# The S5 half of an output projection as seven block products per pair of blocks

## The chip, the cores and the metric

One Trainium2 chip, one of its cores. The metric is the device time of one execution in microseconds (us), as the median of several runs. The engines are TensorE (PE, with its weight loads as PEld), VectorE (DVE), ScalarE (ACT), GpSimd (POOL) and SyncE (SP), whose queue issues nearly all transfers.

## The reference

One layer of a hybrid streaming encoder on 512 prompt frames and 32 sample frames, all float32, model width 2048:

```
h = rmsnorm(x, norm1_g);  p = h @ w_in            # q, f, i, g, u: 1024 columns each
o_h = hgrn_mixer(q, f, i, g)                      # 8 heads of 128, gated linear recurrence
hh  = gelu(s5_scan(u))                            # 64 groups, complex diagonal state
o_s = hh * sigmoid(hh @ w_glu + b_glu)            # the gate
x = x + concat(o_h, o_s) @ w_out                  # the output projection
a = relu(rmsnorm(x, norm2_g) @ w_ff1)             # 2048 x 8192
x = x + a*a @ w_ff2
y = rmsnorm(x, final_norm_g)                      # and the mixers' final states
```

The output projection is a 2048 x 2048 product on 544 frames. Its lower 1024 input channels come from the HGRN heads, its upper 1024 from the gate.

## The kernel before

Activations lie transposed: 128 channels on the partitions, the 544 frames (`T`) along the free axis, in two halves of 272 (`HALF`). A float32 product is made of three products in the type float32r: each operand is split into a high part (a cast on ScalarE) and a low part (the difference, on VectorE), and `step` (L120 on) multiplies high by high, high by low and low by high. `split_w` (L105 on) splits a weight tile of 128 x 1024, `split` an activation of 544 columns.

`gemm` (L128 on) makes one block of 128 output rows: per 8 input blocks a weight tile is loaded into the ring `w`, split into the ring `hl` (two buffers each), and 8 steps for either frame half follow, in two of three PSUM banks `g`. A ring hands out tiles of its pools in turn; a tile waits until all users of the tile before it in that buffer are done. After each second step `tick` lets a piece of other work onto TensorE. The instructions of TensorE stand in the order in which the program writes them; on the other engines a planner orders them, by the place in the program and by its own costs. `first()` moves instructions 2000 places ahead; weight loads and splits use it.

The stages around the change:

- The gate, 8 calls of `gemm` on the S5 output (`ht`, eight split tiles of the pool `a`). Each result becomes `sg` (sigmoid, then a multiplication with `hhl`) and is split into one more tile of pool `a`, kept in `mixs`.
- The S5 half of the output projection (the loop over `NK` = 16 blocks before `drain(0)`): x is loaded in two halves into tiles `xr` of the tag `tt`, `gemm([wo[m, 1]], mixs)` makes the product, VectorE adds it (L1028), and SyncE stores the sum to `x2` in DRAM (L1029).
- Beside it runs `hg_head(7)`, the recurrence of the last HGRN head, a generator whose `yield n` says after how many ticks its next piece may come. Its pieces on TensorE: the transposes of vT (3 ticks) and of kT (24 more for this head), the state products, six levels of diagonal products (5 ticks each), then the output product `po` (L805 on), 3 and 8 ticks later, and a column sum 4 ticks after that. Its exponentials and differences lie on ScalarE and VectorE.
- Each head's normalised output goes to DRAM (`mh`). The loop after `hg_out` loads the eight back into `x_tile("mhl")` and splits them into `mix0` to `mix7` (L1039, L1040). `x_tile` draws on four buffers of the tag `x`, which also hold `hhl` before and x after.
- The HGRN half: 16 calls of `gemm([wo[m, 0]], mixh, ...)`, whose result is added to x; then x is multiplied with the norm's weight and turned into the seven forms that the feed-forward layer takes.

The feed-forward layer's `seven` makes a 2 x 2 block product (two block rows of weights, two frame halves) with seven block products instead of eight, on sums of weight blocks (`s` tiles) and the forms made by `forms`; it has five kinds of PSUM banks for its sums, X, F, C, D and E. Its second half runs 64 such pairs of blocks, each seven products of 4 steps.

Of the kernel before, what the change touches and what calls it, by code (L numbers as in the profile page):

```python
# [37 lines left out]
class Build:  # L38
# [52 lines left out]
    def ring(self, tag, shape=(128, 1024), dt=F32):  # L91

        turn, parts = self.rings[tag]
        self.rings[tag][0] += 1
        turn %= sum(n for _, n in parts)
        for pool, n in parts:
            if turn < n:
                return pool.tile(list(shape), dt, tag=tag, name=tag, bufs=n)
            turn -= n

    def pair(self):
        t = self.ring("hl", (128, 2, 1024), F32R)
        return t[:, 0], t[:, 1]
# [541 lines left out]
    def hg_head(self, h, q, f, vv, g):  # L645
# [35 lines left out]
        for n, (nm, src, wait) in enumerate((("vT", vv, 3), ("kT", kh, 16 if h < 7 else 24))):  # L681
# [74 lines left out]
        for l, hs in enumerate(levels):  # L756
# [6 lines left out]
            yield 5  # L763
# [87 lines left out]
    def mixers(self):  # L851
# [147 lines left out]
        mixs = []  # L999
        for m in range(8):  # L1000
            t = load_hh(m)
            p = self.gemm([d["wg"][m]], ht)
            sg = self.htmp("sg")
            for h in range(2):
                self.tact(sg[:, HALF * h : HALF * h + HALF], p[h], AF.Sigmoid, bias=c["bglu"][:, m : m + 1])
            for s_, o in nat(t):
                v.tensor_mul(jp(sg[:, o]), jp(sg[:, o]), s_)
            mixs.append(self.split(sg))
# [13 lines left out]
        for m in range(NK):  # L1022
            x = [ms.tile([128, HALF], F32, tag="tt", name="xr", bufs=4) for _ in range(2)]
            for h in range(2):
                nc.sync.dma_start(x[h], d["xT"][:, m, HALF * h : HALF * h + HALF])
            p = self.gemm([wo[m, 1]], mixs, (7,) if m == 0 else ())
            for h in range(2):
                add = lambda h=h, x=x, p=p: v.tensor_add(x[h], x[h], p[h])  # L1028
                store = lambda m=m, h=h, x=x: nc.sync.dma_start(self.x2[m][:, HALF * h : HALF * h + HALF], x[h])  # L1029
                adds.append(add) if (m, h) == (NK - 1, 1) else add()  # L1030
                stores.append(store) if m >= NK - 2 else store()
# [3 lines left out]
        for h in range(8):  # L1035
            t = x_tile("mhl")
            nc.sync.dma_start(t, self.mh[h])
            z = ms.tile([128, 2, T], F32R, tag=f"mix{h}", name=f"mix{h}")
# [22 lines left out]
        for k in range(8):  # L1061
            g = []
            for m in (k, k + 8):
                x = x_tile("x")
                nc.sync.dma_start(x, self.x2[m])
                p = self.gemm([wo[m, 0]], mixh, (), late_adds)
# [22 lines left out]
    def forms(self, q, tmp):  # L1089
# [8 lines left out]
        return b11, t1, t2, b21, t3, b22, t4  # L1098

# [351 lines left out]
```

## Time and profile before

| what | us |
|---|---|
| median of 3 runs (2274.66 to 2280.14) | 2278.12 |
| profiled execution | 2274.9 |
| span of its instructions | 2273.1 |
| S5 half of the output projection, 683.75 to 789.70 | 105.95 |
| HGRN half, 789.70 to 885.50 | 95.80 |

Times in a row are counted from the span's start. "Busy" is the time in which at least one instruction of an engine runs. Neighbouring instructions overlap in the profile (a matmul shows 0.29 us and the next begins 0.125 us later), so the time that one takes from its engine is read from start to start. A wait names the instruction whose end released the waiting one.

### The profile page before, as it was taken

The numbers are of one execution on the slowest core, as the hardware profiler recorded it, in microseconds if no ns is written. First come the engines' busy times: TensorE is split into PE (matmuls) and PEld (weight loads), VectorE is DVE, ScalarE is ACT, GpSimd is POOL, SyncE is SP. The second block draws the span as 40 slices with busy tenths as digits, with TensorE's granted clock in tenths as the row PEclk, the third lists the DMA queues.
The fourth block names the chain that finished last, engine by engine and source line by source line (L and its number), as shares of the span: only waits on it lengthen the run. The fifth ranks groups of instructions, "written<-read, shape, count | busy, mean of one in ns | idle before, by whom it ended". The sixth has DMA issues, their size and how long they took to land.

```text
span 2273.1 us, 46802 instructions
## 1 busy us (share of the span) xinstructions
PE 2243.3 (99%) x19318; PEld 2216.2 (97%) x19318; DVE 1800.8 (79%) x2933; ACT 1289.5 (57%) x2267; POOL 39.1 (2%) x59
## 2 busy tenths in 40 slices
PE   8999999999999999999999999999999999999998
PEld 8999999999999999999999999999999999999998
DVE  7988989887656478777777777778888888888896
ACT  5665666564655265555555555556565565565575
POOL 0010001000000000000000000000000000000000
PEclk9999999999999999999999999999999999999999
DMA  5222232222345565445545444447444344344333
GB/s 196 88 87 89 87 90 87 81 89 86 125 146 173 172 191 177 137 157 179 170 166 181 167 154 152 140 149 260 171 163 163 112 162 165 109 162 172 104 102 107
DMA packets 139927, 322.12 MB, mean 142 GB/s; under 512 B 13345, under 2 KB 66337, under 8 KB 139713
## 3 DMA queue, kind: packets, MB, share of 16 engines
q1 hardware_dynamic: 139072, 316.90, 42.4%
q8 instruction: 151, 2.47, 0.4%
q10 hardware_dynamic: 640, 2.23, 0.3%
q14 instruction: 64, 0.52, 0.1%
HBM read 262.21 MB, written 56.87 MB: 140 GB/s over the span
## 4 chain that ended last, share of the span: by engine, by line
PE 90%; DVE 6%; ACT 2%; DMA 1%; issue 1%; SPq 0%; ACTq 0%; DVEq 0%
PE g L124 9%; PE g L126 9%; PE g L125 8%; PE bX L1140 8%; PE bX L1141 8%; PE bX L1142 8%; PE bE L1141 3%; PE bC L1141 3%; PE bE L1140 3%; PE bC L1140 3%; PE bD L1141 3%; PE bD L1140 3%; PE bF L1140 3%; PE bF L1141 3%; PE bD L1142 3%; PE bE L1142 3%
## 5 line engine op out<-in xcount | busy, mean ns | idle before, releaser
L124 PE MATMUL g<-a,hl 128*128 128x272 f32 x1648 | 491.2, 298 | 6.2 <-ACT hl L108 6.2
L126 PE MATMUL g<-a,hl 128*128 128x272 f32 x1648 | 475.7, 289 | 1.3 <-DVE hl L109 1.3
L125 PE MATMUL g<-a,hl 128*128 128x272 f32 x1648 | 474.7, 288 | 0.0
L109 DVE TENSOR_TENSOR hl<-w,hl 128x1024 fp32r<-128x1024 f32 (+3 forms) x348 | 383.7, 1112 | 107.6 <-ACT hl L108 106.4
L108 ACT CAST hl<-w 128x1024 fp32r<-128x1024 f32 (+3 forms) x348 | 334.6, 962 | 198.8 <-PE g L126 113.7
L109 DVE TENSOR_TENSOR hl<-s,hl 128x1024 fp32r<-128x1024 f32 x256 | 313.1, 1223 | 107.8 <-ACT hl L108 107.5
L108 ACT CAST hl<-s 128x1024 fp32r<-128x1024 f32 x256 | 268.7, 1050 | 179.9 <-PE bD L1142 99.7
L124 PEld LDWEIGHTS g<-a,hl 128*128 128x128 f32 x1648 | 311.7, 189 | 11.4 <-ACT hl L108 6.4
L126 PEld LDWEIGHTS g<-a,hl 128*128 128x128 f32 x1648 | 311.0, 189 | 2.0 <-DVE hl L109 2.0
L125 PEld LDWEIGHTS g<-a,hl 128*128 128x128 f32 x1648 | 311.0, 189 | 0.6 <-DVE a L188 0.2
L1141 PE MATMUL bX<-hf,hl 128*128 128x272 f32 x768 | 222.7, 290 | 0.0
L1141 PE MATMUL bX<-f,hl 128*128 128x272 f32 x768 | 222.6, 290 | 0.0
L1140 PE MATMUL bX<-f,hl 128*128 128x272 f32 x768 | 222.3, 289 | 0.3 <-ACT hl L108 0.3
L1140 PE MATMUL bX<-hf,hl 128*128 128x272 f32 x768 | 222.1, 289 | 0.5 <-ACT bD L1133 0.5
L1142 PE MATMUL bX<-f,hl 128*128 128x272 f32 x768 | 221.7, 289 | 0.8 <-DVE hl L109 0.7
L1142 PE MATMUL bX<-hf,hl 128*128 128x272 f32 x768 | 221.3, 288 | 0.0
L1142 PEld LDWEIGHTS bX<-f,hl 128*128 128x128 f32 x768 | 144.5, 188 | 1.2 <-DVE hl L109 1.2
L1140 PEld LDWEIGHTS bX<-hf,hl 128*128 128x128 f32 x768 | 144.7, 188 | 0.7 <-ACT bD L1133 0.7
L1140 PEld LDWEIGHTS bX<-f,hl 128*128 128x128 f32 x768 | 144.7, 188 | 0.6 <-ACT hl L108 0.5
L1142 PEld LDWEIGHTS bX<-hf,hl 128*128 128x128 f32 x768 | 144.6, 188 | 0.0
L1141 PEld LDWEIGHTS bX<-f,hl 128*128 128x128 f32 x768 | 144.4, 188 | 0.0
L1141 PEld LDWEIGHTS bX<-hf,hl 128*128 128x128 f32 x768 | 144.4, 188 | 0.0
(427 smaller groups left out, 5752.5 us busy)
## 6 DMA issues: line engine op xcount, KB each, us to landing
w<-w SPq DMA_DIRECT2D x256, 512.0 KB, 4.0
w<-wi SPq DMA_DIRECT2D x76, 512.0 KB, 3.4
hd<-ft SPq DMA_DIRECT2D x32, 952.0 KB, 4.7
hf<-hd SPq DMA_DIRECT2D x56, 544.0 KB, 6.1
w<-wo SPq DMA_DIRECT2D x32, 512.0 KB, 3.9
x<-x SPq DMA_DIRECT2D x32, 272.0 KB, 2.8
hhl<-hh SPq DMA_DIRECT2D x16, 274.0 KB, 3.5
x<-xT SPq DMA_DIRECT2D x16, 272.0 KB, 5.0
```

What stands on the lines that cost most here:

```text
L108: self.nc.scalar.copy(hi[:, cols], w[:, cols])
L109: self.last_lo = self.nc.vector.tensor_sub(lo[:, cols], w[:, cols], hi[:, cols].bitcast(F32)).ins.name
L124: te.matmul(o, wh, xh, start=k == 0, stop=False)
L125: te.matmul(o, wh, xl, start=False, stop=False)
L126: te.matmul(o, wl, xh, start=False, stop=k == nk - 1)
L1140: nc.tensor.matmul(b[o], wh[:, s], xh, start=start and k == 0, stop=False, skip_group_check=True)
L1141: nc.tensor.matmul(b[o], wh[:, s], xl, start=False, stop=False, skip_group_check=True)
L1142: nc.tensor.matmul(b[o], wl[:, s], xh, start=False, stop=k == nk - 1, skip_group_check=True)
```

## The change

The S5 half is made by seven products for each pair of output blocks. The gate's results stay whole; from the fifth on, result k and result k + 4 are turned into seven right-hand forms (`right_forms`), split into tiles of pool `a`. For each of 8 pairs `left_forms` makes the sums of the two weight tiles and splits them, and `seven_few` runs seven products of 4 steps in three PSUM banks, copying X into C, F and C again and adding the five results to x on the way. It ticks after each second step. x is now loaded two blocks wide into two tiles `x_tile("xr")` a pair.

The rings in this stage take in tiles that are free then: the weights of odd pairs lie in `mix4` and `mix5`, the sums in `mix6` and `mix7`, a third split buffer in pool `a`. Afterwards the old rings are put back. The first call of the HGRN half leaves the steps of blocks 4 to 7 to its end. In head 7 the transposes of kT come 34 ticks after those of vT and each level after 6.

```
-                return pool.tile(list(shape), dt, tag=tag, name=tag, bufs=n)
+                return pool(turn) if callable(pool) else pool.tile(list(shape), dt, tag=tag, name=tag, bufs=n)
...
-        return t[:, 0], t[:, 1]
+        return t if isinstance(t, list) else (t[:, 0], t[:, 1])
...
-        for n, (nm, src, wait) in enumerate((("vT", vv, 3), ("kT", kh, 16 if h < 7 else 24))):
+        for n, (nm, src, wait) in enumerate((("vT", vv, 3), ("kT", kh, 16 if h < 7 else 34))):
...
-            yield 5
+            yield 5 if h < 7 else 6
...
+        mixf = [[None] * 4 for _ in range(7)]
+        b11s = []
+        def right_forms(k):
+            A, B = slice(0, HALF), slice(HALF, T)
+            x, y = mixs[k], mixs[k + 4]
+            if k % 2 == 0:
+                b11s.append(self.atile())
+            ab, cd, ef = b11s[-1], self.atile(), self.atile()
+            gh = self.atile()
+            o = (A, B)[k % 2]
+            fs = self.forms((x[:, A], x[:, B], y[:, A], y[:, B]),
+                            lambda: ms.tile([128, HALF], F32, tag="tt", name="tt", bufs=4))
+            for f, (z, pair, o) in enumerate(zip(fs, (ab, cd, cd, ef, gh, ef, gh), (o, A, B, A, A, B, B))):
+                hi, lo = pair[0][:, o], pair[1][:, o]
+                a.copy(hi, z)
+                v.tensor_sub(lo, z, hi.bitcast(F32))
+                mixf[f][k] = hi, lo
-            mixs.append(self.split(sg))
+            mixs.append(sg)
+            if m > 3:
+                right_forms(m - 4)
-        for m in range(NK):
-            x = [ms.tile([128, HALF], F32, tag="tt", name="xr", bufs=4) for _ in range(2)]
...
+        mt = lambda h: ms.tile([128, 2, T], F32R, tag=f"mix{h}", name=f"mix{h}")
...
+        self.rings["w"] = [0, [(wpool, 2), (lambda n: flat(mt(4 + n)), 2)]]
+        self.rings["s"] = [0, [(lambda n: flat(mt(6 + n)), 2)]]
+        self.rings["hl"] = [1, [(wpool, 2), (lambda n: hl3, 1)]]
+        for i in range(8):
+            m1 = 2 * i
+            xr = [x_tile("xr").rearrange("q (m t) -> q m t", m=2) for _ in range(2)]
+            for h in range(2):
+                nc.sync.dma_start(xr[h], d["xT"][:, m1 : m1 + 2, HALF * h : HALF * h + HALF])
+            with self.first():
+                r1, r2 = self.load_raw(wo[m1, 1]), self.load_raw(wo[m1 + 1, 1])
+            self.seven_few(self.left_forms(r1, r2), mixf, 4, xr, adds if i == 7 else None)
+            for h in (1, 0):
+                for m in range(2):
+                    store = lambda m=m, h=h, xr=xr, m1=m1: nc.sync.dma_start(
+                        self.x2[m1 + m][:, HALF * h : HALF * h + HALF], xr[h][:, m])
                     stores.append(store) if i == 7 else store()
+        self.rings = rings
-                p = self.gemm([wo[m, 0]], mixh, (), late_adds)
+                p = self.gemm([wo[m, 0]], mixh, (4, 5, 6, 7) if m == 0 else (), late_adds)
+    def left_forms(self, r1, r2):
+        v, sp = self.nc.vector, self.split_w
+        L, H = slice(0, 512), slice(512, 1024)
+        s12, s34 = self.ring("s"), self.ring("s")
+        memo = {}
+        def part(key, n, make):
+            if key not in memo:
+                with self.first():
+                    memo[key] = make()
+            return tuple(x[:, 512 * n : 512 * n + 512] for x in memo[key])
+        def m12():
+            v.tensor_add(s12[:, L], r2[:, L], r2[:, H])
+            v.tensor_sub(s12[:, H], s12[:, L], r1[:, L])
+            return sp(s12)
+        def m34():
+            v.tensor_sub(s34[:, L], r1[:, L], r2[:, L])
+            v.tensor_sub(s34[:, H], r1[:, H], s12[:, H])
+            return sp(s34)
+        mr = lambda: sp(r1)
+        return (lambda: part("r", 0, mr), lambda: part("12", 0, m12), lambda: part("12", 1, m12),
+                lambda: part("r", 1, mr), lambda: part("34", 0, m34), lambda: part("34", 1, m34),
+                lambda: part("22", 1, lambda: sp(r2, None, H)))
+    def seven_few(self, left, right, nk, x, last):
+        X, F, C = (self.gbank() for _ in range(3))
+        add = lambda o, p: v.tensor_add(o, o, p)
+        plan = ((X, True, None), (F, True, None), (X, False, C), (C, False, None), (X, False, F), (F, False, None),
+                (C, False, C))
+        for i, (o, start, copy) in enumerate(plan):
+            if copy is not None:
+                with self.first():
+                    a.copy(copy, X)
+            wh, wl = left[i]()
+            for k in range(nk):
...
+                if k % 2:
+                    self.tick()
+            with self.first():
+                if i == 1:
+                    add(x[1], F.unsqueeze(1).broadcast_to([128, 2, HALF]))
+                if i == 3:
+                    add(x[0][:, 0], C)
+                if i == 5:
+                    add(x[1][:, 0], F)
+        def end():
+            return add(x[0][:, 1], C)
+        with self.first():
+            add(x[1][:, 1], X)
+            if last is None:
+                end()
+            else:
+                last.append(end)
```

## Rows read from the trace of the kernel before

**Rows 1.** The page: busy time, share of the span and instructions of each engine.
```profile
PE 2243.3 (99%) x19318; PEld 2216.2 (97%) x19318; DVE 1800.8 (79%) x2933; ACT 1289.5 (57%) x2267; POOL 39.1 (2%) x59
```
**Rows 2.** Stretches: length, busy (instructions) of PE, PEld, DVE, ACT, POOL; clock, DMA share, GB/s.
```profile
683.75:789.70 105.95, 105.95 (x1033) 103.96 (x1032) 62.17 (x113) 42.66 (x74) 0.00 (x0) 1.00 0.52 167
789.70:885.50 95.80, 95.80 (x769) 95.80 (x768) 71.02 (x143) 54.71 (x97) 0.00 (x0) 1.00 0.59 187
```
**Rows 3.** Timeline of VectorE, S5 half: start, duration, instruction, count, idle time before and releaser.
```profile
768.73 0.44 DVE L1028 TENSOR_TENSOR xr<-xr,g 128x272 f32<-128x272 f32 x1 [0.71 <-PE g L126]
...
774.74 0.44 DVE L1028 TENSOR_TENSOR xr<-xr,g 128x272 f32<-128x272 f32 x1 [0.71 <-PE g L126]
```
**Rows 4.** Waits of TensorE in the whole span: total us, times, longest.
```profile
PE ps L805 <- ACT hgAT L793: 3.0, 1, 3.0
```
**Rows 5.** Stretches of the S5 half with head 7, VectorE alone.
```profile
683.75:704.50 20.75, 19.14 (x33) 1.00 0.60 195
704.50:757.83 53.33, 31.98 (x64) 1.00 0.48 149
```
**Rows 6.** The same stretches, weight splits on VectorE (L109) alone.
```profile
683.75:704.50 20.75, 4.89 (x4) 1.00 0.60 195
704.50:757.83 53.33, 8.55 (x7) 1.00 0.48 149
```
**Rows 7.** The same stretches, additions to x (L1028) alone.
```profile
683.75:704.50 20.75, 2.58 (x6) 1.00 0.60 195
704.50:757.83 53.33, 6.50 (x15) 1.00 0.48 149
```
**Rows 8.** Timeline of VectorE, one pair of the second feed-forward layer.
```profile
1629.56 0.69 DVE L1281 TENSOR_TENSOR s<-w 128x512 f32<-128x512 f32 x1
1630.16 0.69 DVE L1286 TENSOR_TENSOR s<-w 128x512 f32<-128x512 f32 x1
...
1633.84 0.43 DVE L1303 TENSOR_TENSOR acc<-acc,bC 128x272 f32<-128x272 f32 x1
1634.18 0.43 DVE L1303 TENSOR_TENSOR acc<-acc,bX 128x272 f32<-128x272 f32 x1
...
1637.84 1.29 DVE L1176 TENSOR_TENSOR hf<-hf 128x1088 fp32r<-128x1088 f32 x1
1639.05 1.22 DVE L109 TENSOR_TENSOR hl<-s,hl 128x1024 fp32r<-128x1024 f32 x1
1640.18 0.68 DVE L1281 TENSOR_TENSOR s<-w 128x512 f32<-128x512 f32 x1
```
**Rows 9.** A stretch of the second feed-forward layer, columns as in rows 2.
```profile
1780.00:1864.00 84.00, 84.00 (x667) 84.00 (x667) 72.94 (x102) 49.64 (x78) 0.00 (x0) 1.00 0.43 148
```
**Rows 10.** The gate's products, columns as in rows 2.
```profile
640.00:684.00 44.00, 44.00 (x354) 44.00 (x353) 23.71 (x32) 20.33 (x33) 0.00 (x0) 1.00 0.45 142
```
**Rows 11.** Timeline of SyncE's queue: start and duration of the issue.
```profile
668.26 0.33 SPq L1037 DMA_DIRECT2D mhl<-mh  x1
...
761.30 0.33 SPq L1037 DMA_DIRECT2D mhl<-mh  x1
...
766.59 0.33 SPq L1025 DMA_DIRECT2D xr<-xT  x1
```
**Rows 12.** Timeline of VectorE around the S5 half.
```profile
685.02 1.26 DVE L1007 TENSOR_TENSOR sg<-sg,hhl 128x512 f32<-128x512 f32 x2
...
752.54 0.72 DVE L225 TENSOR_TENSOR t<-r 128x544 f32<-128x544 f32 x1 [1.42 <-ACT r L58]
...
762.71 0.44 DVE L1028 TENSOR_TENSOR xr<-xr,g 128x272 f32<-128x272 f32 x1 [0.71 <-PE g L126]
...
765.58 0.73 DVE L1040 TENSOR_TENSOR mix<-mhl,mix 128x544 fp32r<-128x544 f32 x1 [2.42 <-ACT mix L1039]
```
**Rows 13.** The page's costliest groups: splits of 1024 columns, busy, mean ns, idle before.
```profile
L109 DVE TENSOR_TENSOR hl<-s,hl 128x1024 fp32r<-128x1024 f32 x256 | 313.1, 1223 | 107.8 <-ACT hl L108 107.5
L108 ACT CAST hl<-s 128x1024 fp32r<-128x1024 f32 x256 | 268.7, 1050 | 179.9 <-PE bD L1142 99.7
```

More of the change, by code (lines that the diff above doesn't have):

```diff
@@ L1020, in late_adds @@
                 self.after(adds.pop(0)(), self.last_lo, "weights first")
-        for m in range(NK):
-            x = [ms.tile([128, HALF], F32, tag="tt", name="xr", bufs=4) for _ in range(2)]
-            for h in range(2):
[L1025 to L1031, printed above, removed]
+        mt = lambda h: ms.tile([128, 2, T], F32R, tag=f"mix{h}", name=f"mix{h}")
+        flat = lambda t: t.rearrange("q a t -> q (a t)")[:, 0:1024].bitcast(F32)
+        hl3 = [self.apool.tile([128, 2, T], F32R, tag="a", name="hl3", bufs=NK) for _ in range(2)]
+        hl3 = [t.rearrange("q a t -> q (a t)")[:, 0:1024] for t in hl3]
+        rings = {t: [0, list(self.rings[t][1])] for t in ("w", "hl")}
+        self.rings["w"] = [0, [(wpool, 2), (lambda n: flat(mt(4 + n)), 2)]]
[4 more added lines that the diff above has]
+            xr = [x_tile("xr").rearrange("q (m t) -> q m t", m=2) for _ in range(2)]
+            for h in range(2):
+                nc.sync.dma_start(xr[h], d["xT"][:, m1 : m1 + 2, HALF * h : HALF * h + HALF])
[6 more added lines that the diff above has]
+                        self.x2[m1 + m][:, HALF * h : HALF * h + HALF], xr[h][:, m])
+                    stores.append(store) if i == 7 else store()
+        self.rings = rings
         self.drain(0)
@@ L1037, in mixers @@
             nc.sync.dma_start(t, self.mh[h])
-            z = ms.tile([128, 2, T], F32R, tag=f"mix{h}", name=f"mix{h}")
+            z = mt(h)
             a.copy(z[:, 0], t)
@@ new lines, in seven_few @@
+    def seven_few(self, left, right, nk, x, last):
+        a, v = self.nc.scalar, self.nc.vector
+        X, F, C = (self.gbank() for _ in range(3))
[8 more added lines that the diff above has]
+            for k in range(nk):
+                s = slice(128 * k, 128 * k + 128)
+                xh, xl = right[i][k]
+                self.nc.tensor.matmul(o, wh[:, s], xh, start=start and k == 0, stop=False, skip_group_check=True)
+                self.nc.tensor.matmul(o, wh[:, s], xl, start=False, stop=False, skip_group_check=True)
+                self.nc.tensor.matmul(o, wl[:, s], xh, start=False, stop=k == nk - 1, skip_group_check=True)
+                if k % 2:
[15 more added lines that the diff above has]
+                last.append(end)
```

## The prediction

> **What bounds the kernel now.** I read the page's first section, then the busy time by stage, then TensorE's list of waits, then VectorE's timeline in the stages that the change touches. TensorE works for 99% of the span and the profiled execution took 2274.9 us, 1.8 us more than its span [rows 1]. The half of the output projection that reads the S5 channels lies from 683.75 to 789.70, the half that reads the HGRN channels behind it to 885.50; TensorE is counted busy in all of both and holds the full clock, granted 1.00 [rows 2]. So a matmul taken out is worth its whole pitch, as long as what feeds TensorE keeps up.
>
> The pitch: undisturbed, one 128-row block of the S5 half (48 matmuls) goes from 768.73 to 774.74, read from its first-half additions, 6.01 us [rows 3]. Sixteen are 96.2 us. Of the stage's 105.95 us, 9.8 are then not this product's: 3.0 are one wait, of head 7's `po` product on the copies into AT (L805 on L793) [rows 4], and 6.8 are head 7's own small products.
>
> Second in line is VectorE. Up to 704.50 it is busy 19.14 of 20.75 us, up to 757.83 31.98 of 53.33 [rows 5]; of this the weight splits are 4.89 and 8.55 [rows 6], the additions to x 2.58 and 6.50 [rows 7]. The rest is head 6's end, head 7 and some splits.
>
> **The change part by part.** Fewer products. Before, 16 blocks of 48 matmuls, 768; after, 8 pairs of blocks, seven products of 4 steps of 3 matmuls, 84 a pair, 672. The second feed-forward layer runs this very form: one pair takes 10.62 us there (from 1629.56 to 1640.18) [rows 8]. Eight are 85.0 us: -11.2 us.
>
> What VectorE must do for it. In the feed-forward layer it is busy 72.94 of 84 us [rows 9], 9.2 us of a pair. Leave out the split of a loaded form (1.21 from its start to the next start, in 7 of 8 pairs: 1.05), add the 544-wide sum into both blocks, which costs about two 272-wide ones less one start (0.34 each [rows 8]), 0.6: about 8.7 us a pair, beside 10.6 of TensorE. Alone that fits, as it does there. ScalarE (49.64 of 84 [rows 9]) has more room.
>
> The additions read PSUM. In SBUF, 512 columns start 0.60 us apart (1629.56 to 1630.16) and 1024 columns 1.13 (1639.05 to 1640.18), so 1.035 ns a column and 0.07 a start, which makes 0.35 for 272; out of PSUM 272 columns start 0.34 apart [rows 8]. The Trainium skill's page "Perfetto Trace Analysis" (section "Optimizing Scalar/DVE Operations") gives VectorE about 125 ns of access to PSUM against 60 to SBUF in every instruction. By the page five additions would cost a pair 0.3 us more, some 2 us over the pairs with head 7; the trace shows no such surcharge, and nothing is added for it.
>
> But head 7 runs beside it. What it takes of VectorE, with head 6's end: up to 704.50, 19.14 - 4.89 - 2.58, less five splits of loaded heads (0.65 from start to start, like the 0.73 of one [rows 12]) and the end of the gate (1.3 and 0.6), 5.1 together, 6.6 us; from there to 757.83, 31.98 - 8.55 - 6.50 = 16.9, of which the last 3.7 (five operations of normalising from 752.54 on [rows 12], for which TensorE does not wait) don't count: 13.2 us. The new right-hand forms also fall to VectorE: each of the four makes 4 differences and 7 low parts of 272 columns, 11 x 0.35 = 3.9 us, less one split of 544 saved for each of eight blocks (0.64). During the gate products VectorE is busy only 23.71 of 44 us [rows 10], so most of that is covered; blocks 4 to 7 would fill it, and the last form can't be made before the last gate product. Without that cover four forms cost 15.4 us. What is left over at 683.75 I bound by 0 and 8 us and take 4.5: the last form without its two early parts (2.8), the gate's last multiplication (1.2 [rows 12]) and half a microsecond.
>
> Now against the ticks. A tick is 6 matmuls, 0.758 us; a pair has 14. The transposes of kT now come at tick 3 + 34 = 37 (before 3 + 24): 28.0 us of products and 0.5 of transposes. VectorE owes by then 37/14 x 8.7 = 23.0, less 3.7 made before 683.75 (a split, four half sums), 6.6 for the heads, 4.5 left over, 1.1 for the next pair: 31.5 against 28.5. TensorE waits 3.0 (0 to 7). From there 34 + 20 more ticks: six levels of 6, then 3, 3, 8 and 4, 54 in all: 40.9 us and 5.5 of small products and the wait of 3.0, 49.4; VectorE owes 54/14 x 8.7 = 33.6 and 13.2, 46.8. It fits, barely: 0.5 (0 to 3). The chain behind the last level keeps its 8 ticks, so the 3.0 us of L805 stays, with 0.5 more from crowding (-3 to +2). 91 of 112 ticks are used, so head 7 ends in time.
>
> The stage's start: product 1 needs the low part of the second split, whose slot comes free only with the last gate product. A cast of 1.05 and a difference of 1.22 [rows 13] end about 2.5 us in, while product 0 lasts 1.5: +1.0 (0 to 2). Queues in order: three PSUM copies a pair on ScalarE must each be done within one product (1.5 us), with casts of 1.05 and head 7's operations ahead of them; behind a late copy stand the next cast and, through it, VectorE. ScalarE is busy for 59% in the layer that has the same copies [rows 9], without a wait to show, so I take +1.0 (0 to 3).
>
> The hand-over, the step I trust least. Today the HGRN heads are loaded and split during the gate, the first load at 668.26 [rows 11], through the four buffers `x`. After, the S5 half keeps its x there, two a pair, and these loads come behind in program order, so heads get buffers only when pair 6's x is stored. From the start of the addition to the next load into a freed buffer 762.71 to 766.59 passed, 3.9 us; from the load of a head to the end of its split 761.30 to 766.31 (765.58 and 0.73), 5.0 [rows 11, 12]. So two buffers come free about 2.4 and 3.9 us into pair 7, two more that long after its end at 10.6. Heads 0 to 3 are then split at 7.4, 8.9, 12.6 and 14.1, 4 to 7 at 17.8, 18.0, 19.3 and 19.5. The first eight steps use heads 0 to 3, so head 3 is late by 1.8 and head 7, due at 14.7, by 4.8 in all, a little less for its high part: +4.5 (0 if the heads get buffers earlier, 6 if SyncE, where wo loads queue behind a waiting head load, adds to it; two prefetched weights cover 6 us of that).
>
> At nothing: xT loads become 16 of 272 KB for 32 of 136 KB, the 32 stores stay, all on SyncE beside products (DMA 0.52 busy [rows 2]); the four late heads need tiles that pair 7 has freed by its fourth product; the first HGRN weights find the two old buffers free, as now. If that cover failed, one load and split, 4 + 2.3 us. POOL is not touched.
>
> Sum: -11.2 + 3.0 + 0.5 + 0.5 + 1.0 + 1.0 + 4.5 = -0.7 us. The profiled 2274.9 would become 2274.2; the median of the runs is 2278.12, 3.2 above that execution, so 2277.4 on its scale. All low ends together give -14, or -11.2 if the wait at L805 stays; all high ends +12.
>
> **The rivals.** (1) VectorE hides it: the list of instructions packs the forms into the gate, heads load early, and only start and queues cost 2 to 3 us: -8.5 us, 2269.6. For it: the feed-forward layer runs the same form with 87% of VectorE and not a visible wait [rows 8, 9]. Against: no head runs there. The Trainium skill's page "Perfetto Trace Analysis" (section "Identifying the Most-Contended Engine") says to improve the most contended engine first and to judge TensorE by its weight loads, 97% here [rows 1]; by that the whole -11.2 would show. (2) VectorE takes the place of TensorE in the first six pairs: the forms are all late (8 left over), so kT waits 7, the levels 2, L805 another 2, start 1, queues 2, the hand-over 5: 19 - 11.2 = +7.8 us, 2285.9. It decides from the point where VectorE's debt at tick 37 passes TensorE's 28.5 us by more than 7. For it: 19.14 of 20.75 busy already [rows 5]. (3) The products don't shrink, a pair taking longer than 10.6 because three PSUM banks serve where the feed-forward layer has eight: a wait of 1 us a pair, 8 on the sum, +7.3 us, 2285.4; against it, each reuse has a product (1.5 us) between.
>
> **How the numbers follow.** Forecast -0.7, its own range -5 to +4.5 us: 0.44. Rival 1: 0.30. Rival 2: 0.20; rival 3: 0.06. What a measurement here can tell is 0.2%, 4.6 us. Faster takes rival 1 and nothing else, 0.30; same 0.45 with a little of the edges; slower 0.25. The range from 2267 (-11.2 us) to 2287 (+9) leaves out under 2 in 10.
>
> **What would show it.** Right: seven-product pairs of 10.6 us in the last two pairs of the S5 half; a wait of some 3 us at the transposes of kT (L685) or in the first pair, on VectorE; L805 still waiting 3; steps of the first HGRN block waiting for `mix` 4 to 5 us in all, with head loads that start after pair 6. Wrong: no wait for `mix` at all (rival 1), or waits of VectorE's at every level (rival 2), or a wait on a PSUM copy in each pair (rival 3).

## The result and the profile after

The changed kernel takes 2309.64 us (median, 2307.56 to 2312.69), the kernel before on the same chip 2276.39 (2274.13 to 2280.14): ratio 1.0148, 95% interval 1.0136 to 1.0160, so 1.5% slower. That lies outside the range of the prediction, on the slow side. The profiled execution took 2309.09 us with a span of 2307.3, 34.2 longer than the span of before. Of the runs below, one of the eight executions of e16_start took 5218.94 us and is left out of its ratio.

The page's first line after, beside [rows 1]: TensorE has 96 instructions fewer and idles for 58 us, where it idled for 30.

```profile
PE 2249.0 (97%) x19222; PEld 2219.4 (96%) x19222; DVE 1848.7 (80%) x3025; ACT 1314.5 (57%) x2327; POOL 39.1 (2%) x59
```

The stretches, columns as in [rows 2] and [rows 10]: the S5 half, now from 685.11 to 809.55, the HGRN half, and the gate's products; the fourth line is the S5 half of before. That half began at 682.60 and ended at 789.56, not at 683.75 and 789.70: gate blocks, 6.01 us each, begin at 670.58 and 676.59, and at 682.60 TensorE takes the next new weight tile. So the gate ends 2.5 us later than in before, the S5 half grew by 17.5 us and the HGRN half by 13.7. TensorE is no longer busy throughout in either, its mean clock is 0.90 and 0.94, and VectorE is busy for 102.41 us of the S5 half where it was 62.17.

```profile
685.11:809.55 124.44, 104.77 (x944) 100.71 (x942) 102.41 (x184) 66.12 (x123) 0.00 (x0) 0.90 0.42 128
809.55:919.20 109.65, 101.61 (x770) 100.60 (x768) 75.35 (x149) 58.31 (x102) 0.00 (x0) 0.94 0.59 186
640.00:684.00 44.00, 44.00 (x353) 44.00 (x352) 26.73 (x48) 18.51 (x37) 0.00 (x0) 1.00 0.35 111
```
```profile
682.60:789.56 106.96, 106.96 (x1041) 104.97 (x1039) 62.17 (x113) 43.60 (x74) 0.00 (x0) 1.00 0.53 168
```

TensorE's waits from 680 to 830, columns as in [rows 4]. Before, it had none at all there; after, 27.7 us, of which two waits of 0.4 and 0.2 at the hand-over are not shown.

```profile
PE g L1180 <- DVE a L1017: 6.0, 1, 6.0
PE ps L805 <- ACT hgAT L793: 4.4, 1, 4.4
PE g L124 <- ACT hl L108: 4.2, 1, 4.2
PE g L124 <- ACT mix L1074: 3.2, 1, 3.2
PE ps L685 <- DVE kh L675: 3.1, 1, 3.1
PE b L729 <- DVE KQ L751: 2.3, 2, 2.1
PE g L1181 <- DVE hl L109: 1.8, 2, 1.0
PE g L1179 <- ACT hl L108: 1.6, 1, 1.6
PE b L773 <- DVE KQ L751: 0.5, 1, 0.5
```

And the clock. These are the stretches between 620 and 1000 in which half of it was granted (0.50, so 1.2 instead of 2.4 GHz); before had none. The one at 689.90 goes with the first pair's waits, the one at 758.20 with a wait of 2.1 us that ends at 756.81 (L729), the one at 782.10 with L805's, those at 812.80 and 823.00 with the hand-over's. The two at 631.90 and 969.80 lie outside the stage, and such stretches also come in kernels without the seven products (e6 at 633.2, e15 at 938.4).

```profile
631.90:638.70 6.80, 6.80 (x31) 6.51 (x31) 1.72 (x3) 2.86 (x5) 0.00 (x0) 0.50 0.64 194
689.90:700.10 10.20, 4.98 (x19) 4.28 (x20) 9.38 (x21) 6.35 (x14) 0.00 (x0) 0.50 0.11 28
758.20:761.60 3.40, 3.40 (x17) 3.40 (x16) 2.26 (x6) 0.93 (x2) 0.00 (x0) 0.50 0.65 218
782.10:792.30 10.20, 9.40 (x40) 9.12 (x41) 1.46 (x2) 3.48 (x8) 0.00 (x0) 0.50 0.00 1
812.80:819.60 6.80, 5.20 (x21) 4.88 (x22) 3.52 (x5) 2.74 (x3) 0.00 (x0) 0.50 0.82 271
823.00:829.80 6.80, 5.50 (x22) 5.19 (x23) 2.31 (x4) 1.91 (x3) 0.00 (x0) 0.50 0.34 107
969.80:973.20 3.40, 3.40 (x18) 3.40 (x17) 0.51 (x1) 1.33 (x2) 0.00 (x0) 0.50 0.31 102
```

What half clock costs is read from TensorE's timeline in the first pair. From 697.38 to 698.06 three matmuls start 0.227 us apart, from 700.46 to 701.95 twelve start 0.124 to 0.125 apart. So of the time that TensorE works at half clock, 1 - 0.125/0.227 = 45% is lost; this is taken for all its work there.

```profile
697.38 0.43 PE L1180 MATMUL g<-a,hl 128*128 128x272 f32 x1
697.61 0.43 PE L1181 MATMUL g<-a,hl 128*128 128x272 f32 x1
...
698.06 0.43 PE L1180 MATMUL g<-a,hl 128*128 128x272 f32 x1
...
700.46 0.28 PE L1181 MATMUL g<-a,hl 128*128 128x272 f32 x1
...
701.95 0.29 PE L1181 MATMUL g<-a,hl 128*128 128x272 f32 x1
```

TensorE's busy time in the seven stretches is 38.7 us, of which 17.4 are lost: 12.8 in the five stretches beside the waits, 4.6 in the other two. With that the span closes: 2307.3 - 27.7 of waits - 17.4 of clock = 2262.2, which is 10.9 us under the 2273.1 of before. The products are cheaper by about what was worked out (11.2); waits took 27.7 and the slower clock 17.4.

Where the first wait comes from, on VectorE: the gate's last multiplication (L1027) runs only at 690.61, behind forms, low parts and a half-sum, and the low part that the first product's fourth step waits for starts at 692.02. [Rows 12] had that multiplication at 685.02.

```profile
690.61 1.16 DVE L1027 TENSOR_TENSOR sg<-sg,hhl 128x512 f32<-128x512 f32 x2
691.67 0.45 DVE L1129 TENSOR_TENSOR tt<-sg 128x272 f32<-128x272 f32 x1
692.02 0.44 DVE L1017 TENSOR_TENSOR a<-sg,a 128x272 fp32r<-128x272 f32 x1
```

And the hand-over, from the S5 half to the HGRN half, on SyncE's queue (as [rows 11]): head 7's store goes out at 803.80, loads of heads that wait for buffers stand behind it from 804.40 on, and the first three weight loads of the HGRN half are issued only at 809.06. TensorE's products of the S5 half end at 809.55.

```profile
803.80 0.32 SPq L827 DMA_DIRECT2D mh<-o  x1
804.40 4.61 SPq L1072 DMA_DIRECT2D mhl<-mh  x3
809.06 1.37 SPq L88 DMA_DIRECT2D w<-wo  x3
```

### The profile page after: what moved, and what is told of

Its sections match the earlier page's. It is cut to its first block, busy times and chain, and to the rows that moved or that the text cites. A ratio compares the mean times of both kernels' runs of the same rounds, so it can differ in the third digit from the quotient of the medians.

```text
span 2307.3 us, 46740 instructions
## 1 busy us (share of the span) xinstructions
PE 2249.0 (97%) x19222; PEld 2219.4 (96%) x19222; DVE 1848.7 (80%) x3025; ACT 1314.5 (57%) x2327; POOL 39.1 (2%) x59
## 4 chain that ended last, share of the span: by engine, by line
PE 86%; DVE 7%; ACT 3%; DMA 2%; issue 1%; SPq 0%; ACTq 0%; DVEq 0%
PE bX L1241 8%; PE bX L1242 8%; PE bX L1243 8%; PE g L124 7%; PE g L126 7%; PE g L125 7%; PE bE L1242 3%; PE bC L1242 3%; PE bE L1241 3%; PE bF L1241 3%; PE bC L1241 3%; PE bD L1242 3%; PE bF L1242 3%; PE bD L1241 3%; PE bD L1243 3%; PE bE L1243 3%
## 5 line engine op out<-in xcount | busy, mean ns | idle before, releaser
L109 DVE TENSOR_TENSOR hl<-w,hl 128x1024 fp32r<-128x1024 f32 (+2 forms) x340 | 371.6, 1102 | 105.0 <-ACT hl L108 104.3
L124 PE MATMUL g<-a,hl 128*128 128x272 f32 x1392 | 417.2, 300 | 6.3 <-ACT hl L108 6.3
L108 ACT CAST hl<-w 128x1024 fp32r<-128x1024 f32 (+2 forms) x340 | 324.5, 955 | 162.6 <-PE g L126 83.6
L126 PE MATMUL g<-a,hl 128*128 128x272 f32 x1392 | 402.9, 289 | 1.3 <-DVE hl L109 1.3
L109 DVE TENSOR_TENSOR hl<-s,hl 128x1024 fp32r<-128x1024 f32 x256 | 312.9, 1222 | 113.6 <-ACT hl L108 113.4
L125 PE MATMUL g<-a,hl 128*128 128x272 f32 x1392 | 402.1, 289 | 0.0
L108 ACT CAST hl<-s 128x1024 fp32r<-128x1024 f32 x256 | 268.7, 1049 | 180.8 <-PE bD L1243 99.7
L124 PEld LDWEIGHTS g<-a,hl 128*128 128x128 f32 x1392 | 264.4, 190 | 11.1 <-ACT hl L108 6.5
L126 PEld LDWEIGHTS g<-a,hl 128*128 128x128 f32 x1392 | 263.8, 190 | 2.0 <-DVE hl L109 2.0
L125 PEld LDWEIGHTS g<-a,hl 128*128 128x128 f32 x1392 | 263.8, 189 | 0.6 <-DVE a L188 0.2
```

The lines of the kernel that those rows point to most:

```text
L108: self.nc.scalar.copy(hi[:, cols], w[:, cols])
L109: self.last_lo = self.nc.vector.tensor_sub(lo[:, cols], w[:, cols], hi[:, cols].bitcast(F32)).ins.name
L124: te.matmul(o, wh, xh, start=k == 0, stop=False)
L125: te.matmul(o, wh, xl, start=False, stop=False)
L126: te.matmul(o, wl, xh, start=False, stop=k == nk - 1)
```

## The experiments

Two theories stood at first. A: a few single waits, each paid again by the clock. C: VectorE has too much to do, so that a wait taken away comes back elsewhere. The runs were made on several chips, each beside executions of before on its own chip, so the ratios are what to compare. "Waits" below is TensorE's sum from 680 to 830 in us, "clock" 45% of its busy time in the half-clock stretches from 620 to 1000, "rest" the profiled span less both.

| run | us | ratio to before (95%) | waits | clock | rest |
|---|---|---|---|---|---|
| before | 2276.39 | 1 | 0 | 0 | 2273.1 |
| after | 2309.64 | 1.0148 (1.0136 to 1.0160) | 27.7 | 17.4 | 2262.2 |
| e1_fill | 2305.90 | 1.0132 (1.0115 to 1.0149) | 16.7 | 11.8 | 2263.2, less 15.1 of fillers |
| e2_early | 2300.43 | 1.0111 (1.0096 to 1.0126) | 23.0 | 12.9 | 2263.5 |
| e3_own | 2296.79 | 1.0098 (1.0083 to 1.0113) | 23.8 | 11.9 | 2263.5 |
| e4_po | 2298.24 | 1.0102 (1.0087 to 1.0117) | 22.8 | 9.7 | 2264.1 |
| e5_all | 2291.51 | 1.0060 (1.0040 to 1.0079) | 18.7 | 6.8 | 2264.4 |
| e7_nospread | 2304.76 | 1.0126 (1.0105 to 1.0146) | 27.8 | 12.2 | 2262.8 |
| e8_start_end | 2295.12 | 1.0084 (1.0066 to 1.0103) | 19.1 | 12.2 | 2264.9 |
| e9_best | 2288.54 | 1.0055 (1.0040 to 1.0070) | 15.9 | 5.9 | 2266.2 |
| e10_direct | 2285.00 | 1.0043 (1.0029 to 1.0058) | 14.4 | 5.9 | 2262.9 |
| e12_pool | 2290.67 | 1.0066 (1.0051 to 1.0081) | 18.9 | 7.1 | 2263.6 |
| e13_pool_gate | 2291.38 | 1.0069 (1.0054 to 1.0084) | 18.0 | 10.8 | 2263.0 |
| e16_start | 2283.41 | 1.0035 (1.0023 to 1.0046) | 13.6 | 8.3 | 2263.1 |
| e18_start_pool34 | 2288.93 | 1.0056 (1.0040 to 1.0072) | 13.8 | 10.6 | 2264.0 |
| e14_nosums | 2279.40 | 1.0019 (1.0010 to 1.0029) | 10.3 | 5.8 | 2262.0 |
| e17_start_nosums | 2277.24 | 1.0008 (0.9998 to 1.0018) | 8.2 | 4.6 | 2263.1 |
| e6_before_spread | 2275.97 | 1.0005 (0.9995 to 1.0014) | 0 | 3.1 | 2272.1 |
| e11_before_wait | 2289.26 | 1.0059 (1.0044 to 1.0074) | 12.0 | 3.3 | 2273.0 |
| e15_before_load | 2278.24 | 1.0013 (1.0003 to 1.0022) | 1.7 | 1.5 | 2273.6 |

The last column is the main reading: every kernel that makes the half as before, in 16 blocks, has 2272 to 2274, every one with seven products a pair 2262 to 2266, whatever the waits. With the waits and the half clock of the whole span taken off, also outside these windows, the two groups lie closer together in themselves, 2251 to 2252 and 2241 to 2243: the products save 9 to 10 us by that account.

**The clock.** e1 put matmuls whose results go nowhere into the gaps; e11 put one wait into the kernel before, and nothing else.

```
e1:  def fill(self, n, x): ... matmul(t, x[:, 0:128], x) n times   # 40, 30, 30, 20 of them
e11: if m == 13:  # before, S5 half
         v.tensor_copy(z, p[1]); 16 times v.tensor_tensor(z, z, z, ALU.max)
         self.stop = matmul(pst, ones, z)        # the next step's first matmul comes behind it
```

> The changed kernel with filler matmuls on a scratch bank in its four long waits: 40 (5.0 us at full clock) before the first pair's fourth step, 30 before head 7's output product, 30 ahead of the HGRN half, 20 ahead of its ninth step. They take nothing away from the waits and are a little shorter than these. Theory A (the waits cost twice: by their length and because TensorE's clock falls to 0.5 behind them): the half-clock stretches near 690, 782, 813 and 823 go, the waits stay about as long, 8 to 13 us faster than the changed kernel, about 2299. Rival B (the clock is a by-product, the loss is VectorE's work alone): no change or up to 5 us slower, 2309 to 2314.

Measured: the first pair's 6.0 us became filler (0.7 is left, and the 1.6 and 1.0 behind it are 1.9 and 1.3), and the half-clock stretches at 690 and 782 are gone; others came at 699.8 and 730.5, and the hand-over's stays. In all 30.7 us from 620 to 1000 instead of 47.8. By the ratios the gain is 3.6 us, not clear of noise (the intervals overlap): the fillers (120 by 0.125, 15 us) take the room of what they save.

> The clock's price by itself: the kernel before with one single wait of TensorE put in, at the end of the 14th step of the S5 half, where before has none: a small matmul that stands behind a chain of 17 VectorE operations on 272 columns (0.39 us each, about 6.6 us) which starts with that step's last product; its result goes nowhere. Theory A (a wait of this size is paid twice, by its length and by half clock behind it): wait 6 to 7 us, a stretch at 0.50 of 6.8 to 10.2 us behind it, so 10 to 12 us in all, ratio 1.0044 to 1.0053. Rival (a wait costs its length and the half clock in the changed kernel has another cause): the clock stays at 1.00 and the span grows by 6.5 to 7.5 us, 1.003.

TensorE's wait in e11, and its half-clock stretch:

```profile
PE ps L1035 <- DVE z L1034: 12.0, 1, 12.0
```
```profile
780.30:794.00 13.70, 3.94 (x15) 3.71 (x16) 10.12 (x22) 0.65 (x1) 0.00 (x0) 0.50 0.43 149
```

The wait was 12.0 us, not 6.6: VectorE put other operations between the links of the chain. Work had stopped at 778.04, half clock was granted from 780.30, and the full clock came back at 794.00, 3.9 us after work went on at 790.06. So this wait does bring half clock, as theory A says; but most of the stretch lies inside the wait, where it costs nothing, and only 3.94 us of work fall into it (1.8 us lost; a stretch of 3.4 at 951.0 lost 1.5). The span grew by 15.2 us, of which the wait is four fifths. This wait is not paid twice.

**The waits, one by one.**

```
e2: forms of x alone (b11, t1) made in results 0 to 3:  if m > 3: right_forms(m - 4)  else: early_forms(m)
e3: xr of pairs 0 to 6 in rpool "raw", not x_tile("xr"), the two in reversed order
e4: yield 8 -> yield 8 if h < 7 else 18        # ahead of po
e5: e2 + e3 + e4
```

> The changed kernel, with the two forms that need only results 0 to 3 (b11 and b12-b11) made and split as soon as that result is there, where VectorE was idle. Theory A: the 6.0 us wait in the first pair shrinks to 0 to 3 us (what is left is for b22 and b21 of the last result) and the clock there holds longer: 5 to 9 us faster, about 2302. Rival C (VectorE is over-full for the whole of head 7, so a wait taken out at one place comes back at the next): kT's wait grows from 3.1 to 6 or more, 0 to 3 us faster, 2307 or more.

> The changed kernel, with x of pairs 0 to 6 in three free buffers of the tag raw in place of the tag x, so that the HGRN heads can be loaded and split during the S5 half as before the change. Theory A: of the 8 us of waits at the hand-over those for mix (3.2 and 0.2) go; the one for the first HGRN weights stays in part, since their load stands behind head 7's on SyncE: 3 to 8 us faster with the clock behind it, about 2304. Rival C: no gain, the heads' splits only move work into the stretch where VectorE is full, 2308 to 2313.

> The changed kernel, with head 7's output product 18 ticks behind the last level in place of 8. Theory A: its wait (4.4 us) and the half clock behind it (782 to 792) go, but head 7's output is stored up to 7 us later and its load holds up the weights behind it at the hand-over: 2 to 6 us faster, about 2305. Rival C or a hand-over that takes all of it back: within 2 us, 2308 to 2312.

> The three edits of the runs before in one kernel: the forms of x alone made in results 0 to 3, pairs 0 to 6 of xT in the other tiles in reversed order, and head 7's second scores 10 ticks later. One by one they gave -8.4 us (early forms, 1.0111), -11.4 us (own tiles, 1.0098) and -10.4 us (later scores, 1.0102) against the 2305.7 us that 1.0136 to 1.016 of this chip's before would be. Theory A (the loss is a handful of single waits, each paid again by a slower clock behind it): they act at three places, so the gains add nearly whole: about -25 us, ratio 0.999 to 1.005. Theory C (VectorE has too much to do in this stage, so a wait taken away comes back at the next place): the sum is little better than the best of them: ratio 1.007 to 1.010.

Each removed the wait that it aimed at. In e2 the wait for form b11 went, but at the start of the next product 7.0 us for the cast of the first half-sum (ScalarE, L108) took over, and the transposes' 3.1 shrank to 0.3; in e3 the waits for `mix` went, and the transposes' grew to 4.7; in e4 L805's 4.4 went, and `mix` rose to 5.9. By the ratios the three gave 8.4, 11.4 and 10.5 us alone, 30.3 in sum, and 20.0 together, at a ratio (1.0060) between what the two theories gave. Both hold in part: clock and waits fall together, and some waits move.

```
e7:  the changed kernel with 24 and 5 ticks for head 7, as before
e6:  the kernel before with 34 and 6 ticks
e10: e5, and head 7's result is cast from o_ into mix7, without mh
e8:  e5, the first pair's left operands and the last sigmoid ahead of the last forms; loads of mhl 5 to 7 behind the first wo
e16: e10 with e8's start only
```

> The changed kernel with the old ticks of head 7 (24 and 5), the seven products kept. If the spread is part of what brings the loss (it puts the scores at L805 and the last store of mh later, so the hand-over waits): 5 to 10 us faster than after, 1.010 to 1.012. If it helps, as meant (the first pairs have fewer other operations to share VectorE with): 3 to 8 us slower than after, 1.016 to 1.018. Theory A says the L805 wait stays (the sum behind it still stands behind the next pair's parts) and the kT wait grows from 3.1 to 5 or more, with a half-clock stretch behind each.

> The kernel before with only the spread of head 7 taken over (34 ticks ahead of the transposes of k, 6 a chunk), no seven products. The prediction's view: the spread by itself changes nothing or little, since head 7 has 192 ticks and uses 91 of them in before: 0.999 to 1.001. Rival: the later head costs the hand-over, since mhl 7 comes later: +2 to +5 us, 1.001 to 1.002.

The spread alone does nothing to before. In the changed kernel it cut the transposes' wait from 7.7 to 3.1 us, but po's products, which wait 1.0 and 1.8 in e7, wait 4.4 with it; the sum of waits is the same, and e7's lower time, by overlapping intervals not clear of noise, comes with less half clock.

> e5 with one edit more: head 7's result is cast straight into its tile, and is neither stored to mh nor loaded from it. In e5 SP stood 11.6 us at that store, and the loads of the first HGRN weights were issued right behind it, at 799.6; they were cast 4.5 us later, and TensorE waited 5.7 us. If SP's queue is what makes the hand-over wait, the wait shrinks to under 1.5 us and the half-clock stretch of 6.8 us behind it goes: 6 to 9 us faster than e5, ratio 1.002 to 1.004. Rival: the first weights wait for memory that the S5 half's tiles leave (the last addition of the last pair), so SP gains 1 us or less: ratio 1.005 to 1.006.

> e5 plus two more moves: the first pair's loads and its first two left operands made ahead of the last result's forms, with the last sigmoid and multiplication put first; and the loads of mhl 5 to 7 put behind the load of the first HGRN weights on SP. In the run with early forms the first pair still waited 7.0 us for s12's cast on ScalarE and the hand-over 4.1 us for the first weights. Theory A: both go or shrink to under 2 us, and with them one or two half-clock stretches of 10.2 and 6.8 us: 10 to 15 us faster than e5, ratio 0.992 to 0.999, so faster than before. Theory C: the forms are late in the first pair's products 2 to 6 instead, at the same total: within 3 us of e5.

> e10 with the first pair's loads and its first two left operands made ahead of the last result's forms, and the last sigmoid and multiplication put first (the start of e8, with the hand-over of e10). If the wait of the first pair is one of order on ScalarE, it goes from 8.3 us (7.0 and 1.3) to 3 to 5 as in e8; if VectorE's load is what sets the end, the transposes of k wait longer for it (2.4 to some 5 us). Expected: 0 to 4 us faster than e10's 2285.0, ratio 1.0025 to 1.0045; slower than before all the same.

In e10 the first weights are issued at 786.77 instead of behind head 7's store, and the hand-over's wait for them fell from e5's 5.7 to 1.3 us: SyncE's queue was its cause. e8 only moved other loads, and is no faster than e5: its hand-over still waits 5.2 and 2.7. Its start did shrink, but the transposes then waited 5.2. e16 has the same two sides: the first pair waits 2.2, 1.2 and 2.5 in place of e10's 7.0 and 1.3, and the transposes 5.2 in place of 2.4.

TensorE's waits in e10, then in e16:

```profile
PE g L1202 <- ACT hl L108: 7.0, 1, 7.0
PE ps L685 <- DVE kh L675: 2.4, 1, 2.4
```
```profile
PE ps L685 <- DVE kh L675: 5.2, 1, 5.2
PE g L1209 <- ACT a L1013: 2.5, 1, 2.5
PE g L1209 <- ACT hl L108: 2.2, 1, 2.2
```

e9 rearranged the whole gate (results in the order 0, 4, 1, 5, 2, 6, 3, 7, forms as early as tiles are free, 40 and 16 ticks) beside e10's edits:

> What the runs before point to, in one kernel: gate results in the order 0, 4, 1, 5, 2, 6, 3, 7 with the forms of a pair of results made as soon as both are there, the last gate product with its k loop outside (so that its operand tiles come free one by one), the first pair's left operands ahead of the last forms, own tiles for pairs 0 to 6 of xT, 40 ticks ahead of the transposes of k, 16 ahead of the second scores, and head 7's result cast straight into its tile instead of through mh, so that neither SP's store nor its load of it stands ahead of the next half's first weights. e5 had 2291.5 us with 8.2 us of waits in the first pair, 2.7 for the transposes, 5.7 at the hand-over and 27.3 us at half clock, of which the stretches in these stages cost about half their length. Theory A (single waits, each paid again by the clock): these go or halve, 15 to 25 us faster than e5: ratio 0.995 to 1.000. Theory C (VectorE over-full): forms and parts of weights late in the first pairs all the same: 1.004 to 1.007.

Its first pair waits 3.8 us in all (not the 5 that e13's expectation gives), but its transposes 7.7 and the hand-over 4.0: no better than e10, and inside the range of theory C.

**VectorE's load.**

```
e14: e10;  m12: return sp(r2);  m34: return sp(r1)         # no half-sums
e17: e16 with the same
e15: before, after the additions of blocks 0 to 14, in first():  6 times v.tensor_tensor(z, x[1], x[1], ALU.max)
e12: e10;  m12, m34: g.tensor_add, g.tensor_sub, g = nc.gpsimd
e13: e9 with 34 ticks and the same;  e18: e16 with m34 alone on GpSimd
```

> e10 with the half-sums left out altogether: the raw weights are split in their place (the products then have other operands, of the same number and size). VectorE is relieved by 19.5 us, ScalarE and TensorE do what they did. Theory C: as the better case of e12, 1.000 to 1.0025, VectorE's busy time from 690 to 790 down from 92 to some 75 us. Theory O: 1.004 to 1.005.

> The kernel before with six VectorE operations more (272 columns, 0.35 us each) in each of the first 15 steps of the S5 half, behind that step's additions: 31.5 us in all, that no other engine waits for; the products stay 16 by 6.01 us. VectorE's load in the half comes to about what the seven products bring. Theory C: the waits of the changed kernel appear (transposes of k, second scores, hand-over): +4 to +10 us, ratio 1.002 to 1.0045, some half clock. Theory O: the same time as before, 0.999 to 1.001.

> e16 with the half-sums of the weights left out as in e14 (raw weights are split in their place; the products have other operands of the same number and size). VectorE has room and the first wait is short. If the seven products save what was worked out (11.2 us on TensorE) and only these waits ate it, the time falls below before: 2268 to 2274, ratio 0.997 to 0.9995. If something unseen is dearer, it stays at 1.001 to 1.002 as e14.

The middle of the S5 half in e10, e14 and e15, columns as in [rows 2], for the last two with TensorE's longest waits behind it.

```profile
690.00:790.00 100.00, 93.39 (x884) 90.18 (x885) 89.26 (x157) 55.81 (x105) 0.00 (x0) 0.94 0.48 157
```
```profile
690.00:790.00 100.00, 96.35 (x930) 93.24 (x930) 78.81 (x137) 59.36 (x112) 0.00 (x0) 0.98 0.51 164
```
```profile
PE g L1198 <- ACT hl L108: 6.1, 2, 5.9
PE g L124 <- ACT hl L108: 2.6, 1, 2.6
```
```profile
690.00:790.00 100.00, 98.34 (x967) 95.93 (x966) 88.96 (x196) 36.67 (x63) 0.00 (x0) 1.00 0.53 168
```
```profile
PE ps L685 <- DVE kh L675: 1.5, 1, 1.5
```

Without the half-sums the transposes wait for nothing (nor do they in e12, where GpSimd makes them), and by the ratios 5.5 us are gained, so C is right that VectorE's work sets those waits; the first pair's 5.9 us stays. But e15, with VectorE as busy as in e10, costs 3 us and waits 1.7: load alone is not it. What differs is what the work is for: in e10 VectorE also makes the operands of the next products (low parts of forms and of sums), so that its delays can reach TensorE. That is the likely reading; no run tests it alone. e17, with the shortest waits of all, comes to the time of before and not below: 8.2 us of waits and 4.6 of clock remain, some 13 us against the 10 that the products save.

> e10 with the four half-sums of each pair's weights (512 columns each, 0.61 us on VectorE, so 2.4 us a pair and 19.5 us in the half) moved to GpSimd, where nothing runs in this half. Theory C (VectorE is over-full): the wait for the transposes of k (2.4 us in e10) and the later ones of 1.4 and 1.3 go, 4 to 8 us faster than e10's 2285.0, ratio 0.9995 to 1.0025. Theory O (only the order in the queues): the first pair's 7.0 us for s12's cast stays and so do the others, 1.004 to 1.005. A third: GpSimd takes several us for each and slows VectorE by sharing SBUF with it; then the products wait for s12 and s34, 1.006 and more.

> e9 with the half-sums on GpSimd and 34 ticks instead of 40 ahead of the transposes. e9 had 5 us of waits in the first pair and 7.7 for the transposes, with VectorE busy 96% from 680 to 730. Theory C: VectorE gains 2.4 us a pair, by 730 some 10 us; the 7.7 us wait goes to under 2, and with it 10.2 us at half clock, most of which lie beside the wait: 6 to 9 us faster than e9's 2288.5, ratio 1.0015 to 1.003; hand-over 4 us still there. Theory O: the wait stays where it is, 1.005.

> e16 with only the second pair of half-sums (s34, needed five products later) on GpSimd. GpSimd took 1.65 to 1.97 us for each in e12 against 0.68 on VectorE, so 3.4 us a pair, which 6 us of products cover; VectorE is relieved by 1.2 us a pair, 9.8 us in all. If the casts of s34 on ScalarE keep standing ahead of the copies of banks (e12's four waits of 1 to 1.9 us), no gain: 1.003 to 1.006. If not: 1.001 to 1.003.

Moving the sums to GpSimd gained nothing: e12, e13 and e18 came out 0.14 to 0.23% above e10, e9 and e16, with intervals that overlap a little. GpSimd's operations in e12 (two of eight groups), then VectorE's groups of splits and scans; the third fence is e10; the last shows two of e12's four splits, and the GpSimd half-sum beside the second:

```profile
L1173 POOL TENSOR_TENSOR mix<-mix 128x512 f32<-128x512 f32 x4 | 7.9, 1966 | 22.6 <-DMA mix<-wo 16.5 <-DVE hl L109 6.1
L1173 POOL TENSOR_TENSOR mix<-w 128x512 f32<-128x512 f32 x4 | 5.5, 1365 | 151.6 <-DMA w<-wo 136.2 <-DMA x<-xr 8.9 <-DVE hl L109 6.4
```
```profile
L109 DVE TENSOR_TENSOR hl<-w,hl 128x512 fp32r<-128x512 f32 x4 | 3.5, 866 | 0.0
L669 DVE TENSOR_TENSOR_SCAN G<-ones,raw 128x128 f32<-128x128 f32 x4 | 4.0, 1044 | 0.0
```
```profile
L109 DVE TENSOR_TENSOR hl<-w,hl 128x512 fp32r<-128x512 f32 x4 | 2.7, 686 | 0.0
```
```profile
734.96 0.68 DVE L109 TENSOR_TENSOR hl<-w,hl 128x512 fp32r<-128x512 f32 x1
787.36 1.43 DVE L109 TENSOR_TENSOR hl<-w,hl 128x512 fp32r<-128x512 f32 x1
785.98 2.27 POOL L1179 TENSOR_TENSOR mix<-mix,mix 128x512 f32<-128x512 f32 x1
```

By its group a half-sum takes 1.37 to 1.97 us there against 0.68 on VectorE. The mean of VectorE's splits, 866 ns for 686, is three of 0.68 us and one of 1.43 that ran beside a half-sum. In e12 the first pair's wait for s12's cast grew from 7.0 to 9.9 us, and TensorE waits 5.3 us in four places for copies of banks on ScalarE; in e13 and e18 the transposes still wait 4.5 and 4.6. Of the seven-product kernels that compute the whole, the fastest is e16, 0.35% slower than before; none beats it.

## Why the prediction was wrong

- **Fewer products, -11.2: right.** The rest column gives -10.9 for the change itself, the account over the whole span 9 to 10 us. Pair 1, the only one with neither a wait nor half clock, took 10.51 us.
- **The clock: no term.** "A matmul taken out is worth its whole pitch, as long as what feeds TensorE keeps up" set the condition and gave no price for its failing. It cost 17.4 us, half of the loss; 12.8 of it lies beside the new waits. A wait brings it on (e11), and with fillers in their place the stretches at 690 and 782 are gone (e1).
- **The start, +1.0 (0 to 2): 8.6** (6.0, 1.6 and 1.0). I counted one cast and one difference after the gate, and not that the last result's multiplication, the forms of two results and the half-sums stand in the same queues (692.02 above). The 4.5 us "left over" were charged to the transposes alone, 28 us on, when the first product meets them first.
- **kT, +3.0 (0 to 7): 3.1.** Right in place, and the size is luck. The transposes came 43.9 us after the first product, and VectorE was busy for 41.9 of them, where 31.5 were worked out against 28.5 of TensorE; TensorE had already lost 8.6 us at the start and 2.2 of clock. The work left over from the gate (forms and the last multiplication), taken as 4.5 (0 to 8), was 8.5 behind 685.11. e7 shows that the spread is worth 4.6 us there.

```profile
685.11:729.04 43.93, 32.25 (x235) 31.09 (x233) 41.90 (x77) 28.79 (x57) 0.00 (x0) 0.88 0.46 144
```

- **Levels, +0.5: 2.8. L805, +0.5: 4.4.** And a misreading: the 3.0 us of [rows 4] stand at 631.15, in head 6's second scores, 51 us ahead of this stage. In before, head 7's came without a wait, so the whole 4.4 is new, and all of that stage's time that is not the 16 blocks (10.8 us with its right ends) was head 7's small products. e4 removed the wait by ticks.

```profile
631.15 0.38 PE L805 MATMUL ps<-hgAT,vT 128*128 128x128 f32 x1 [2.95 <-ACT hgAT L793]
```

- **The hand-over, +4.5 (0 to 6): 8.1**, of which `mix` 3.4, near what was priced. The other 4.7 are the first HGRN weights, which stood "at nothing", with 4 + 2.3 us if that cover failed. It failed in SyncE's queue (e10): I had weight loads queue behind a head load, but counted two as prefetched, and the first three were issued at 809.06, when the S5 products ended.
- **ScalarE's queues, +1.0:** no wait for a bank copy shows in the changed kernel; rival 3 has nothing for it.

A last 0.8 us is a wait for a split in pair 7 (L1181), which had no term. The sum of the measured waits, 27.7, against the 10.5 of the prediction is 17 us, and the clock another 17. Rival 2 came nearest in kind: VectorE has TensorE's place at the start, but not at every level, and its 7.8 us were short for the same two reasons. The Trainium skill's rule for the engine to improve ("Perfetto Trace Analysis", section "Identifying the Most-Contended Engine") would have given the whole -11.2. The measurement decides otherwise: weight loads were 97% busy [rows 1] and the products did give 10.9, and yet the span rose by 34.2 us, through waits and clock. The PSUM surcharge that the Trainium skill gives ("Perfetto Trace Analysis", section "Optimizing Scalar/DVE Operations") stays unseen: after, additions out of PSUM take 432 ns for 272 columns and low parts out of SBUF 442.

```profile
L1168 DVE TENSOR_TENSOR xr<-xr,g 128x272 f32<-128x272 f32 x24 | 10.4, 432 | 2.4 <-PE g L1181 1.9 <-ACT g L1174 0.3
L1017 DVE TENSOR_TENSOR a<-tt,a 128x272 fp32r<-128x272 f32 x5 | 2.1, 442 | 0.0
```

That the gate ends 2.5 us later in the changed kernel is half clock too: the stretch at 631.90 cost 3.1 us. In e16 two such stretches ahead of the gate's end cost 5.8 us, and it ends 5.0 later; in e14 there is none, and it ends at 682.60 as in before. Open is why head 6's wait, 2.9 to 3.0 us in before and after, is followed by half clock in some kernels (6.8 us here, 10.2 in e16, and 6.8 in e6, which has no seven products) and by none in before.

## What to carry to other kernels

Where TensorE has not one wait, a saving on it is paid out only if every operand of the new form is ready in time: add up the other engines' work by the moment it is due, at the first product above all, not by the stage. Price each new wait with the clock behind it (here some 13 us of clock beside 28 of waits). And look at what stands in front of a load in its queue when a producer moves to the end of a stage.

## What the runs showed of the hardware

GpSimd and VectorE slow each other where both take two operands from SBUF. In e12, beside half-sums on GpSimd, VectorE's scans of 128 columns took 1044 ns in the mean, against 406 in the changed kernel without them, and a split of 512 columns 1.43 us, against 0.68 for the three that had no half-sum beside them. Additions of 272 columns with one input in PSUM took 428 ns beside half-sums and 426 without. Of GpSimd's half-sums, two that met no VectorE instruction took 1.29 and 1.31 us, the longest of the others 3.3. The Trainium skill's page "SBUF — State Buffer" (section "SBUF: two separate sides") has a port pair that the two engines share, held for a whole instruction, which VectorE needs when it reads two inputs from SBUF; these rows agree with it. The clock had two levels only, 1.00 and 0.50, in all 20 traces; in e11's long wait it fell 2.3 us after the last product, and was back 3.9 us after work went on.
